# Making the pool of small columns ahead of the pools for weights in a two-block f32 kernel

## The chip, the cores and the metric

The kernel runs on one core of one Trainium2 chip (trn2). The metric is the device time of one execution in microseconds; it is given as the median of several runs. One execution was also taken by the hardware profiler, and every row below is from that one.

## The reference, cut to what matters

Sequence 512, model width 1024, all inputs and weights f32. A first block has an even layer (input projection, a 31-tap causal convolution, multi-scale pooling, output projection) and an odd layer (a gated linear recurrence over 12 heads of 128 channels). A second block has an S5 layer with a gated output projection, an MLP and a gated side input, then an attention layer with a window of 128 and a second MLP and side input. What matters here is that nearly all of it is matrix products of 512 tokens with weights that are used once:

```python
p = jnp.einsum("btd,dn->btn", h, w_in)                      # even and odd layer
y = jnp.einsum("btn,nd->btd", y, w_out)
ab = y @ w_glu                                              # S5 layer
h = h + jnp.square(jax.nn.relu(hm @ w_up[i])) @ w_down[i]   # both layers of the second block
gate = jax.nn.sigmoid(rmsnorm_2(h, norm_ple[i]) @ w_ple_gate[i])
```

## The kernel before

Activations lie in SBUF with channels on the 128 partitions and 512 tokens along the free dimension. To keep f32 accuracy with f32r matmuls, every activation and every weight is held as a pair `hi`, `lo` with hi + lo equal to the f32 value, and each product is three matmuls (`mm3`, L279 to L286): hi weights with the hi activation (L284), hi weights with the lo activation (L285), lo weights with the hi activation (L286). The weights are the stationary operand (128 columns of 4 bytes, so 512 bytes per partition) and the activation is streamed (512 columns, 2048 bytes per partition). One output tile of 128 channels with 1024 inputs is 8 times `mm3`, 24 matmuls on one PSUM bank (`mtile`).

Weights come in chunks of 128 x 1024 floats, in an order that `queue_w` lays down for the whole program. `prep` (L256 to L269) does one chunk: SP issues the DMA into a tile of pool `raw` (2 slots), ScalarE copies it to a tile of pool `whi` (tag `hi`, 3 slots, L266), and VectorE or GpSimd subtracts into a tile of pool `wlo` (tag `lo`, 3 slots, L268). `get_w` runs it up to three chunks ahead of the matmuls that use them.

SBUF is handed out by pools. Seven pools live for the whole program and are made in `Kern.__init__` (L171 to L178): `const`, `raw`, `whi`, `wlo`, `h` (the residual stream), `xg` (normed activations, 16 tiles of 2048 bytes) and `small` (columns of statistics: tags `v`, `rs`, `st`, `sm`, of 4 to 24 floats, 4 slots each). Pools lie one behind the other in the order in which they are made. Behind them each phase opens a pool of its own, whose tiles are made by `self.L(tag, ...)`; that pool is given back when the phase ends, and the next phase's pool begins at the same place. In the kernel before, the pools begin at these bytes of a partition:

| pool | begins at | size | remainder of its tiles by 512 |
|---|---|---|---|
| raw | 21056 | 8192 | 64 |
| whi | 29248 | 12288 | 64 |
| wlo | 41536 | 12288 | 64 |
| h | 53824 | 20480 | 64 |
| xg | 74304 | 32768 | 64 |
| small | 107072 | 1152 | - |
| phases | 108224 | - | by the tag, below |

The size of `small` is 4 slots of 32 + 64 + 96 + 96 bytes. All other pools of the list have sizes that are multiples of 512 bytes.

What each phase streams against the weights (the time is where it stands in the profiled execution):

- even layer, 0 to 430 us: `xg`, and from the phase's pool `big` and `d`
- odd layer, 430 to 722 us: `xg`, `xs` against two small weight tiles `wrh` and `wrl` of the same phase's pool, then `y` for its output projection
- S5, 722 to 806 us: small matmuls of 64 columns; the projections of the side inputs (`y`) fill PE's idle time
- gated output projection (`glu`), 806 to 892 us: `y`. Two of its sixteen chunks aren't in `whi` and `wlo` but, since L1251, in the phase's tiles `x` and `gt`
- MLP and, behind it, the side input with its gate (`ple`), twice (892 to 1294 us, and 1493 to 1897 us): products with `w_up` stream `xg`, those with `w_down` and `w_gate` stream `hid`; each half of the hidden width is 16 output tiles of `w_up`, then 8 of `w_down` with 2048 inputs each
- attention, 1294 to 1493 us: `xg`, then `o` for queries and part of the output projection; scores and values use `q`, `k`, `pt`, `vh`, `vl` of the phase's pool among themselves

PE runs its matmuls in program order; each phase's order is fixed when the program is built.

Of the kernel before, what the change touches and what calls it, by code (L numbers as in the profile page):

```python
# [37 lines left out]
class Vecs:  # L38
    def __init__(self):
        self.parts, self.at, self.n = [], {}, 0  # L40
# [116 lines left out]
class Kern:  # L157
# [10 lines left out]
    def __init__(self, ctx, tc, I, O, vat, cat):  # L168
        self.tc, self.nc, self.I, self.O = tc, tc.nc, I, O
        self.vat, self.cat = vat, cat  # L170
        P = lambda name, bufs, **k: ctx.enter_context(tc.tile_pool(name=name, bufs=bufs, **k))  # L171
        self.p_const = P("const", 1)
        self.p_raw = P("raw", 2)
        self.p_hi = P("whi", 3)
        self.p_lo = P("wlo", 3)
        self.p_h = P("h", 10)
        self.p_xg = P("xg", 16)
        self.p_s = P("small", 4)  # L178
        self.ps_st = P("stats", 1, space=PSUM)
        self.dram = P("dram", 1, space=bass.MemoryType.DRAM)  # L180
        self.chunks, self.prepped, self.next_prep, self.next_get = [], {}, 0, 0
# [1565 lines left out]
```

## Time and profile before

| | us |
|---|---|
| median of 3 runs | 1912.23 |
| lowest, highest | 1911.62, 1917.79 |
| the profiled execution's own time | 1913.36 |
| its span, from the first to the last instruction | 1911.6 |

The span is 1.8 us shorter than the time of the same execution. Times in the rows are microseconds, and the duration of a single instruction (mean) is in nanoseconds. A matmul's duration reaches from its start to the modelled end of its last result; matmuls overlap, so 24 matmuls that each last 390 ns take much less than 24 times 390 ns, and what a matmul costs in a dense stretch is the distance from its start to the next one's start. I call that distance its step. It can be read in two ways: from the starts in the timeline, or from a stretch in which PE is never idle, as the length of the stretch plus one duration, divided by the count of matmuls that touch it (the plus is for the ones that the stretch cuts at its ends). PEclk 1.00 is the full TensorE clock (2.4 GHz), 0.5 the lower level (1.2 GHz).

### The profile page before, as it was taken

The numbers are of one execution on the slowest core, as the hardware profiler recorded it, in microseconds if no ns is written. First come the engines' busy times: TensorE is split into PE (matmuls) and PEld (weight loads), VectorE is DVE, ScalarE is ACT, GpSimd is POOL, SyncE is SP. The second block draws the span as 40 slices with busy tenths as digits, with TensorE's granted clock in tenths as the row PEclk, the third lists the DMA queues.
The fourth block names the chain that finished last, engine by engine and source line by source line (L and its number), as shares of the span: only waits on it lengthen the run. The fifth ranks groups of instructions, "written<-read, shape, count | busy, mean of one in ns | idle before, by whom it ended". The sixth has DMA issues, their size and how long they took to land.

```text
span 1911.6 us, 23182 instructions
## 1 busy us (share of the span) xinstructions
PE 1777.6 (93%) x8530; PEld 1427.3 (75%) x8530; DVE 1256.9 (66%) x1940; ACT 751.2 (39%) x1274; POOL 573.4 (30%) x606
## 2 busy tenths in 40 slices
PE   6998989799988797799999999999999999999997
PEld 5776767567766675687888888887778888888886
DVE  8999999976778768755432344478776642244456
ACT  3334332443454553224432332334665432233234
POOL 4889877683657643200000000023000000000002
PEclk8999989898989898899999999999999999999998
DMA  4233333432212378623232222333111222222322
GB/s 151 85 112 98 101 100 117 119 95 90 75 63 88 110 238 279 203 77 111 93 99 89 100 99 89 100 105 111 49 54 45 100 99 89 98 100 90 98 88 94
DMA packets 104289, 200.57 MB, mean 105 GB/s; under 512 B 26736, under 2 KB 57072, under 8 KB 104176
## 3 DMA queue, kind: packets, MB, share of 16 engines
q1 hardware_dynamic: 96496, 182.41, 29.7%
q0 software_dynamic: 2640, 8.65, 1.4%
q10 hardware_dynamic: 5040, 8.04, 1.2%
q8 instruction: 67, 1.10, 0.2%
q14 instruction: 46, 0.38, 0.1%
HBM read 176.38 MB, written 22.02 MB: 104 GB/s over the span
## 4 chain that ended last, share of the span: by engine, by line
PE 62%; DVE 21%; issue 5%; POOL 5%; DMA 4%; ACT 3%; SPq 1%; ACTq 0%; POOLq 0%; DVEq 0%
PE mm L284 17%; PE mm L285 17%; PE mm L286 17%; DVE cv L240 7%; POOL lo L228 2%; DVE pl L228 1%; PE pv L1519 1%; DMA raw<-in_w_in_odd 1%; DVE srr L228 1%; ACT hi L225 1%; PE sc L284 1%; PE sc L285 1%; PE sc L286 1%; DVE xs L228 1%; DVE lo L228 1%
## 5 line engine op out<-in xcount | busy, mean ns | idle before, releaser
L225 ACT ACTIVATE hi<-raw 128x1024 fp32r<-128x1024 f32 (+1 forms) x280 | 292.5, 1047 | 674.8 <-PE mm L285 541.4
L228 DVE TENSOR_TENSOR lo<-raw,hi 128x1024 fp32r<-128x1024 f32 (+1 forms) x185 | 227.2, 1228 | 417.7 <-ACT hi L225 414.3
L286 PE MATMUL mm<-xg,lo 128*128 128x512 f32 x924 | 365.7, 396 | 5.6 <-POOL lo L228 5.6
L284 PE MATMUL mm<-xg,hi 128*128 128x512 f32 x924 | 366.4, 398 | 1.7 <-ACT xs L225 1.4
L285 PE MATMUL mm<-xg,hi 128*128 128x512 f32 x924 | 365.0, 396 | 0.0
L1333 POOL DMA_DIRECT2D pj<-proj x16 | 8.8, 549 | 1036.3 <-DVE t L240 795.7
L228 POOL TENSOR_TENSOR lo<-raw,hi 128x1024 fp32r<-128x1024 f32 (+1 forms) x95 | 233.5, 2460 | 127.0 <-ACT hi L225 116.3
L284 PE MATMUL mm<-hid,hi 128*128 128x512 f32 (+1 forms) x648 | 254.4, 393 | 1.4 <-DVE t L228 1.4
L285 PE MATMUL mm<-hid,hi 128*128 128x512 f32 (+1 forms) x648 | 253.9, 392 | 0.0
L286 PE MATMUL mm<-hid,lo 128*128 128x512 f32 (+1 forms) x648 | 253.8, 392 | 0.0
L286 PEld LDWEIGHTS mm<-xg,lo 128*128 128x128 f32 x924 | 176.4, 191 | 44.5 <-POOL lo L228 7.1
L284 PEld LDWEIGHTS mm<-xg,hi 128*128 128x128 f32 x924 | 176.6, 191 | 41.1 <-ACT xs L225 1.9
L285 PEld LDWEIGHTS mm<-xg,hi 128*128 128x128 f32 x924 | 176.7, 191 | 38.4 <-issue 1.2
L240 DVE SCALAR_TENSOR_TENSOR cv<-b,hw,cv 128x510 f32<-128x510 f32 (+28 forms) x232 | 159.0, 729 | 0.0
L284 PEld LDWEIGHTS mm<-hid,hi 128*128 128x128 f32 x648 | 121.7, 188 | 30.2 <-DVE t L228 1.6
L286 PEld LDWEIGHTS mm<-hid,lo 128*128 128x128 f32 x648 | 121.7, 188 | 28.6
L285 PEld LDWEIGHTS mm<-hid,hi 128*128 128x128 f32 x648 | 121.7, 188 | 28.5
L284 PE MATMUL mm<-y,hi 128*128 128x512 f32 x192 | 79.3, 413 | 8.9 <-ACT y L225 8.4
L285 PE MATMUL mm<-y,hi 128*128 128x512 f32 x192 | 77.5, 404 | 0.0
L286 PE MATMUL mm<-y,lo 128*128 128x512 f32 x192 | 77.0, 402 | 0.0
L285 PE MATMUL mm<-big,hi 128*128 128x512 f32 x160 | 67.8, 425 | 8.7 <-DVE big L240 7.9
L284 PE MATMUL mm<-big,hi 128*128 128x512 f32 x160 | 65.0, 425 | 5.3 <-DVE gt L240 3.0
(467 smaller groups left out, 3140.9 us busy)
## 6 DMA issues: line engine op xcount, KB each, us to landing
raw<-in_w_up SPq DMA_DIRECT2D x64, 512.0 KB
raw<-in_w_down SPq DMA_DIRECT2D x64, 512.0 KB
raw<-in_w_in_even SPq DMA_DIRECT2D x40, 512.0 KB
raw<-in_w_in_odd SPq DMA_DIRECT2D x24, 512.0 KB
raw<-in_w_out_even SPq DMA_DIRECT2D x16, 512.0 KB
raw<-in_w_glu SPq DMA_DIRECT2D x16, 512.0 KB
raw<-in_w_gate SPq DMA_DIRECT2D x16, 512.0 KB
raw<-in_w_out_odd SPq DMA_DIRECT2D x16, 384.0 KB
```

Source lines behind the costliest of these rows:

```text
L225: self.nc.scalar.activation(out=out, in_=in_, func=func, scale=scale, bias=bias)
L228: (eng or self.nc.vector).tensor_tensor(out=out, in0=a, in1=b, op=op)
L240: self.nc.vector.scalar_tensor_tensor(out=out, in0=a, scalar=s, in1=b, op0=op0, op1=op1)
L284: mm(out, hi[:, sl], xh, start=start, stop=False)
L285: mm(out, hi[:, sl], xl, start=False, stop=False)
L286: mm(out, lo[:, sl], xh, start=False, stop=stop)
L1333: self.nc.gpsimd.dma_start(out=p, in_=pj[m])
L1519: mm(o, l, r[:, w], start=n == 0, stop=n == 6 * nk - 1)
```

## The change

The line that makes the pool `small` moves from behind the pool `xg` to behind the pool `const`.

```diff
         self.p_const = P("const", 1)
+        self.p_s = P("small", 4)
         self.p_raw = P("raw", 2)
         self.p_hi = P("whi", 3)
         self.p_lo = P("wlo", 3)
         self.p_h = P("h", 10)
         self.p_xg = P("xg", 16)
-        self.p_s = P("small", 4)
         self.ps_st = P("stats", 1, space=PSUM)
```

No instruction is added, removed or moved in the code. `small` then begins where `raw` began, and `raw`, `whi`, `wlo`, `h` and `xg` begin 1152 bytes later, which is 2 x 512 + 128; the phases' pools begin at 108224 as before. The remainder by 512 of the tiles of these five pools goes from 64 to 192. That of the phases' tiles stays, by the sizes of what lies ahead of them in their pool: 192 for `xs`, `wrh`, `wrl`, `x`, `gt`, `y` and `hid`, 448 for `d` and `o`, 32 for `big`. Slices of a weight tile begin at multiples of 512 bytes in it, and streamed tiles are 2048 bytes each, so the distance between a streamed tile and a slice of weights has one remainder by 512 for each pair of tags:

| streamed | weights | before | after |
|---|---|---|---|
| xg | hi, lo | 0 | 0 |
| xs | wrh, wrl | 0 | 0 |
| y | x, gt | 0 | 0 |
| y | hi, lo | 128 | 0 |
| hid | hi, lo | 128 | 0 |
| d, o | hi, lo | 384 | 256 |
| big | hi, lo | 480 | 352 |

## Rows read from the trace of the kernel before

**Rows 1.** The page's first part: busy time, share of the span, instructions of each engine.
```profile
PE 1777.6 (93%) x8530; PEld 1427.3 (75%) x8530; DVE 1256.9 (66%) x1940; ACT 751.2 (39%) x1274; POOL 573.4 (30%) x606
```

**Rows 2.** Stretches by phase: busy us (instructions) of PE, PEld, DVE, ACT, POOL; clock; DMA.
```profile
0.00:430.00 430.00, 376.24 (x1621) 291.78 (x1622) 409.78 (x713) 165.72 (x343) 335.65 (x438) 0.93 0.35 109
...
638.00:722.00 84.00, 78.22 (x330) 61.86 (x329) 60.25 (x56) 39.38 (x55) 43.64 (x32) 0.96 0.64 201
722.00:806.00 84.00, 59.79 (x878) 48.83 (x879) 73.47 (x144) 20.24 (x37) 26.64 (x23) 0.86 0.78 253
806.00:892.00 86.00, 84.65 (x378) 68.45 (x374) 36.51 (x45) 25.01 (x33) 1.65 (x3) 1.00 0.28 94
...
981.00:1071.00 90.00, 90.00 (x388) 72.40 (x387) 20.91 (x18) 21.80 (x26) 0.00 (x0) 1.00 0.30 94
1071.00:1158.00 87.00, 87.00 (x385) 72.07 (x384) 39.27 (x46) 34.23 (x48) 0.00 (x0) 1.00 0.29 97
...
1294.00:1493.00 199.00, 190.16 (x1048) 153.84 (x1048) 150.67 (x329) 118.40 (x311) 16.43 (x15) 0.98 0.21 68
```

**Rows 3.** Waits of ScalarE, 978 to 1296 us: total us, times, longest.
```profile
ACT hi L225 <- PE mm L285: 173.7, 50, 4.6
```

**Rows 4.** PE alone, inside stretches of one streamed tag: length, busy (matmuls), clock, DMA.
```profile
985.00:1065.00 80.00, 80.00 (x345) 1.00 0.31 97
1075.00:1155.00 80.00, 80.00 (x354) 1.00 0.28 95
...
1590.00:1670.00 80.00, 80.00 (x344) 1.00 0.29 94
1675.00:1755.00 80.00, 80.00 (x355) 1.00 0.29 99
...
825.00:885.00 60.00, 60.00 (x260) 1.00 0.31 106
```

**Rows 5.** Groups by line and form, 806.5 to 890.6 us: count, busy us, mean ns.
```profile
L285 PE MATMUL mm<-y,hi 128*128 128x512 f32 x105 | 41.4, 395 | 0.0
...
L285 PE MATMUL sp<-y,x 128*128 128x512 f32 x8 | 3.1, 390 | 0.0
L285 PE MATMUL sp<-y,gt 128*128 128x512 f32 x8 | 3.1, 390 | 0.0
```

**Rows 6.** Timeline of PE, first and last of 24 matmuls in a row, and the next.
```profile
817.66 0.39 PE L284 MATMUL sp<-y,x 128*128 128x512 f32 x1
...
822.88 0.40 PE L286 MATMUL sp<-y,gt 128*128 128x512 f32 x1
823.11 0.40 PE L284 MATMUL mm<-y,hi 128*128 128x512 f32 x1
```

**Rows 7.** Groups by line and form, PE, whole span: count, busy us, mean ns, idle.
```profile
L284 PE MATMUL mm<-hid,hi 128*128 128x512 f32 x632 | 249.8, 395 | 0.0
...
L285 PE MATMUL mm<-y,hi 128*128 128x512 f32 x192 | 77.5, 404 | 0.0
...
L285 PE MATMUL mm<-big,hi 128*128 128x512 f32 x160 | 67.8, 425 | 8.7 <-DVE big L240 7.9 <-DVE big L228 0.8
...
L285 PE MATMUL mm<-o,hi 128*128 128x512 f32 x56 | 22.0, 394 | 0.0
...
L285 PE MATMUL sc<-o,hi 128*128 128x512 f32 x40 | 15.9, 398 | 0.0
...
L285 PE MATMUL sp<-y,hi 128*128 128x512 f32 x24 | 10.4, 433 | 0.0
...
L285 PE MATMUL yp<-y,hi 128*128 128x512 f32 x24 | 9.5, 395 | 0.0
...
L285 PE MATMUL mm<-d,hi 128*128 128x512 f32 x16 | 6.3, 393 | 0.0
L284 PE MATMUL mm<-hid,hi 128*128 128x256 f32 x16 | 4.6, 289 | 1.4 <-DVE t L228 1.4
```

**Rows 8.** Chain of waits, 638 to 722 us: shares by line.
```profile
by line: issue 7.3%; DMA raw<-in_w_proj 7.0%; PE sp L286 6.4%; DVE e L733 6.0%; POOL lo L228 5.8%; PE sp L284 5.6%; PE sp L285 5.4%; PE mm L286 5.0%; PE yp L285 5.0%; PE yp L286 5.0%; PE mm L285 5.0%; PE yp L284 5.0%; PE mm L284 5.0%; ACT x
```

## The prediction

> **What bounds the kernel now.** I read the page's busy times first, then the stretches phase by phase, then the waits, and last the steps of single matmuls. PE is busy 93% of the span [rows 1], but that is an average over phases with different limits [rows 2]. In the even layer (0 to 430 us) PE is busy 376 of 430 us while VectorE is busy 410: VectorE sets the pace there. In S5 (722 to 806 us) PE is idle 24 of 84 us. From 806 us on it is otherwise: in the gated output projection PE is busy 84.7 of 86 us, in the stretches of the MLPs 90.0 of 90 and 87.0 of 87 us at the full clock of 2.4 GHz, with VectorE at a quarter to a half of its time. There the time of the kernel is the count of matmuls times the step from one to the next. Nothing else is late: ScalarE, which makes the `hi` weights, mostly waits for PE to give a weight buffer back, 173.7 us between 978 and 1296 us [rows 3]. So weights lie ready ahead of PE, and a PE with a shorter step finishes sooner.
>
> The step isn't the same everywhere. I take stretches in which only one streamed tag runs and PE has no idle time [rows 4]. With `hid` streamed, 345 and 344 matmuls touch 80 us; with `xg`, 354 and 355. A matmul lasts about 0.39 us, so the step is (80 + 0.39)/345 = 233.0 ns and 80.39/344 = 233.7 ns for `hid`, 233.4 ns on average, and 227.1 and 226.5 ns, 226.8 on average, for `xg`. Same form of matmul, same weight pools, same clock, about the same DMA rate (94 to 99 GB/s): 6.6 ns apart, in both layers. For `y` in 825 to 885 us it is 60.39/260 = 232.3 ns.
>
> What tells `hid` and `y` from `xg` is, by the table of the change, the distance to the weights: a multiple of 512 bytes for `xg`, 128 more for the others. The trace has a control inside one phase: in the gated output projection 48 matmuls stream `y` against weights that lie in `x` and `gt`, at a multiple of 512. Twenty-four of them in a row start between 817.66 and 822.88 us [rows 6]: 23 steps in 5.22 us, 227.0 ns. Right behind them the same tiles of `y` against `hi` and `lo` go at 232.3 ns. The durations say the same: 390 ns against `x` and `gt`, 395 against `hi` [rows 5]. So it isn't the streamed tile, and since `xg` goes at 226.8 with `hi` and `lo`, it isn't the weights' pool either; it is the pair.
>
> **The change part by part.** It removes and adds no instruction, wait or buffer, and moves none past a queue: sizes of pools, and so the reuse of their slots, stay. It moves five pools by 1152 bytes. What that can change is what depends on addresses; I price it by streamed tag.
>
> `hid`: 632 matmuls on each of three lines [rows 7], 1896, go from a distance of 128 to 0. If they take the step of `xg`: 1896 x 6.6 ns = 12.5 us. All of it lies on the path, since PE is never idle there [rows 2]. If they gain only what `y` shows between its two kinds of weights, 232.3 - 227.0 = 5.3 ns, it is 10.0 us. I take 12.5, from the stretches of the same kind and length, and keep 10.0 for the range.
>
> `y`: 3 x (192 + 24 + 24) = 720 matmuls against `hi` and `lo` [rows 7], also from 128 to 0. In the gated output projection 105 per line [rows 5], 315 x 5.3 ns = 1.7 us, on the path since PE has 1.4 us of idle time in 86. In 638 to 722 us PE runs 330 matmuls, nearly all of them `y`: 312 x 5.3 ns = 1.6 us at most. But PE is idle 5.8 of 84 us there, the clock is 0.96, and the chain of waits has loads of weights with 7% and GpSimd's `lo` with 6% [rows 8], which don't get shorter, so 0 to 1.6; I take the middle, 0.8. The rest, 720 - 315 - 312 = 93, fills idle time of PE in S5: nothing.
>
> `xg`, `xs`, and `y` against `x` and `gt` keep the distance 0: nothing.
>
> `o`, `d` and `big` change from one distance that isn't 0 to another: 384 to 256, 384 to 256, 480 to 352. No row shows 256 or 352. The rows nearest to them are those at 128 and 384: `o` lasts 394 ns and `d` 393, `hid` 395 [rows 7], so the penalty hardly depends on the distance once there is one, and I take 0. From both sides: `o` has 3 x (56 + 40) = 288 matmuls, which could lose the whole penalty or pay it twice, 288 x 6.6 ns = 1.9 us either way. `big` has 3 x 160 and `d` 3 x 16, 528 x 6.6 ns = 3.5 us, but in a phase where VectorE sets the pace, so at most half, 1.7 us either way.
>
> VectorE, ScalarE and GpSimd also read and write tiles that move against each other, such as `h` against the phases' tiles; the pair that they handle most, `raw` with `hi` into `lo`, moves together and keeps its distances. No row lets me price the others; where it would count, behind 806 us, these engines have slack [rows 2], so 0.
>
> Sum: 12.5 + 1.7 + 0.8 = 15.0 us. The profiled execution took 1913.4 us, so 1898.4; it stands 1.1 us above the median of the runs, 1912.2, and from that it is 1897.2 us. Ends: 12.5 + 1.7 + 1.6 + 1.9 + 1.7 = 19.4 us gained, 1892.8; and 10.0 + 1.7 + 0 - 1.9 - 1.7 = 8.1 us gained, 1904.1. With a microsecond for the spread of the runs: 1892 to 1905.
>
> **A rule that speaks against it.** In this trace the same `y` tiles go at 227.0 ns against one set of weights and at 232.3 against the other [rows 4, 6], so what the weights are, or where they lie, reaches into the step of the streaming matmul. The Trainium skill, TensorE: Matmul & The Clock Gate, section Step-by-step: what each phase is for, says that PE has two independent read ports into SBUF, one for the streamed operand and one for the weight load, and that loading the next weights takes no read bandwidth from the running matmul. By that rule a distance between the two addresses would be worth nothing and the time would stay at 1912; the rows don't agree with it by 5 to 7 ns a matmul.
>
> **The rivals.** First, *the pair matters, but not by the remainder of 512*. All pairs at 227 ns are also near neighbours in SBUF (`xg` with `hi` and `lo`, `y` with `x` and `gt`), all slow pairs lie farther apart; a slower step for far tiles would fit rows 4 to 6 as well. The change leaves far tiles far: the sum is 0 and the time 1912. Nothing in the rows rules it out; against it is only that the penalty would have to step once at some place and then stay flat. The skill's rule of independent ports ends at the same time.
>
> Second, on the other side, *what counts is where a tile lies by itself*: tiles of `raw` to `xg` at remainder 64 are the good ones, and the change takes them to 192. Then `xg` against `hi` and `lo` would go from 226.8 to 233.4 ns: `w_up` alone has 2 layers x 32 tiles x 24 = 1536 matmuls in stretches where PE is never idle, 1536 x 6.6 ns = 10.1 us, and the time would be 1922. It decides from the first `w_up` tile on. Against it: `y`, `x` and `gt` all lie at 192 and go at 227.0 ns [rows 6].
>
> Third, *the gain on `hid` is given back*: with steps of 227 ns a chunk of weights is used up in 24 x 227 = 5.4 us instead of 5.6, and loads or conversions become late. Against it: the stretches of `xg` use chunks at just that rate, with VectorE busy 39 of 87 us instead of 21 of 90, and PE stays at 87.0 of 87 [rows 2]. Were most of the 12.5 us eaten, the time would be about 1908.
>
> **How the numbers follow.** The forecast has 0.87; the rival of near and far 0.06, with no change; the weights that come late 0.03, also inside 0.3%; tiles by themselves 0.04, slower. 0.3% is 5.7 us, about what a measurement of this kernel can tell from no change; the forecast's whole range lies beyond it. So faster 0.87, same 0.09, slower 0.04. The range of the forecast holds nearly all of its 0.87, and I leave the rivals' times out of it.
>
> **What would show it.** Right, if in the profile of the changed kernel 80 us inside a stretch of `hid` hold 353 to 355 matmuls, with 389 or 390 ns each, the stretches of `xg` still hold 354, the 24 matmuls against `x` and `gt` still take 5.2 us and those behind them the same step; and if the even layer and attention end as late after their start as now, within 2 us. Wrong, if `hid` stays at 344, or if `xg` falls to 344, or if PE shows idle time inside a stretch of `hid`.

## The result and the profile after

The changed kernel takes 1901.11 us (median, 1900.59 to 1902.89) where the kernel before takes 1911.92 beside it: a ratio of 0.9936, with a 95% interval of 0.9918 to 0.9953. It was timed twice more, each time beside the kernel before: 0.9953 (0.9936 to 0.9970; 1904.50 against 1915.36 us) and, in five rounds, 0.9929 (0.9917 to 0.9941; 1902.78 against 1916.24 us). So it is faster by 0.5 to 0.7%, by the ratios 9 to 14 us. Forecast were 15.0 us and 1897.2, with a range of 1892 to 1905. Ratios leave out executions in a slow state, of which there was one in all the runs below (4376.7 us, with the gap of 128 bytes). All engines run the same instructions in the same order in both kernels; only addresses differ.

First the stretches of PE inside one streamed tag, which answer to [rows 4]: length, busy time (matmuls), clock, DMA. The first, third and fourth are `hid`, the second and fifth `xg`, and the last, from the gated output projection, `y`.

```profile
985.00:1060.00 75.00, 75.00 (x333) 1.00 0.30 97
1075.00:1145.00 70.00, 70.00 (x311) 1.00 0.29 98
1165.00:1240.00 75.00, 75.00 (x333) 1.00 0.30 96
1580.00:1655.00 75.00, 75.00 (x332) 1.00 0.31 99
1670.00:1740.00 70.00, 70.00 (x310) 1.00 0.28 98
...
825.00:885.00 60.00, 60.00 (x267) 1.00 0.31 106
```

By the same reading as before, `hid` has a step of 75.39/333 = 226.4 and 75.39/332 = 227.1 ns, where it had 233.0 and 233.7. `xg` stays: 70.39/311 = 226.3 and 70.39/310 = 227.1 ns. `y` goes from 232.3 to 60.39/267 = 226.2 ns. The groups of the gated projection (807 to 889 us; count, busy us, mean ns), which answer to [rows 5], show it in the durations: `y` against `hi` now lasts as long as against `x` and `gt`.

```profile
L285 PE MATMUL mm<-y,hi 128*128 128x512 f32 x103 | 40.1, 389 | 0.0
...
L285 PE MATMUL sp<-y,x 128*128 128x512 f32 x8 | 3.1, 389 | 0.0
...
L285 PE MATMUL sp<-y,gt 128*128 128x512 f32 x8 | 3.1, 389 | 0.0
```

Then the timeline of PE, the matmuls that answer to [rows 6]: 23 steps from 819.24 to 824.45 us, 226.5 ns, where it was 227.0. But the last of them starts 1.57 us later than before (822.88).

```profile
819.24 0.39 PE L284 MATMUL sp<-y,x 128*128 128x512 f32 x1
...
824.45 0.39 PE L286 MATMUL sp<-y,gt 128*128 128x512 f32 x1
824.68 0.39 PE L284 MATMUL mm<-y,hi 128*128 128x512 f32 x1
```

Where the time went is read from the starts of the blocks. Of the kernel before, the first `hid` of the first MLP, the first `xg` behind it, the next first `hid`, and the first matmul of attention:

```profile
981.15 0.40 PE L284 MATMUL mm<-hid,hi 128*128 128x512 f32 x1
...
1070.74 0.39 PE L284 MATMUL mm<-xg,hi 128*128 128x512 f32 x1
...
1157.79 0.40 PE L284 MATMUL mm<-hid,hi 128*128 128x512 f32 x1
...
1293.81 0.39 PE L284 MATMUL sc<-xg,hi 128*128 128x512 f32 x1
```

The same four of the changed kernel:

```profile
981.09 0.39 PE L284 MATMUL mm<-hid,hi 128*128 128x512 f32 x1
...
1068.12 0.39 PE L284 MATMUL mm<-xg,hi 128*128 128x512 f32 x1
...
1155.16 0.39 PE L284 MATMUL mm<-hid,hi 128*128 128x512 f32 x1
...
1287.61 0.39 PE L284 MATMUL sc<-xg,hi 128*128 128x512 f32 x1
```

From each to the next: 89.59 us of `hid` become 87.03, 87.05 us of `xg` stay 87.04, and 136.02 us of `hid` become 132.45. The second MLP repeats it (89.59 and 87.04). The whole account of the profiled executions, from starts of blocks in the timelines:

| part | before, us | after, us | difference |
|---|---|---|---|
| start to the first `y` of the odd layer's output projection | 638.19 | 640.26 | +2.07 |
| from there to the last of the 24 matmuls of [rows 6] | 184.69 | 184.19 | -0.50 |
| the rest of the gated output projection, 300 of its 336 matmuls against `hi` and `lo` | 69.22 | 67.58 | -1.64 |
| `w_up`, four blocks together | 352.09 | 352.06 | -0.03 |
| `w_down` of the first halves, two blocks | 179.18 | 174.07 | -5.11 |
| `w_down` of the second half and side input, first MLP | 136.02 | 132.45 | -3.57 |
| attention | 199.39 | 200.29 | +0.90 |
| `w_down` of the second half, side input and the end, to the last matmul | 144.99 | 142.41 | -2.58 |

The sum is -10.5 us. The rows with `hid` and the gated projection together give 12.9; 2.5 are lost ahead of the 24 matmuls and in attention.

### The profile page after: what moved, and what is told of

Its sections match the earlier page's. It is cut to its first block, busy times and chain, and to the rows that moved or that the text cites. A ratio compares the mean times of both kernels' runs of the same rounds, so it can differ in the third digit from the quotient of the medians.

```text
span 1901.1 us, 23182 instructions
## 1 busy us (share of the span) xinstructions
PE 1758.7 (93%) x8530; PEld 1425.8 (75%) x8530; DVE 1259.9 (66%) x1940; ACT 749.7 (39%) x1274; POOL 571.0 (30%) x606
## 4 chain that ended last, share of the span: by engine, by line
PE 57%; DVE 23%; issue 6%; DMA 5%; POOL 4%; ACT 3%; SPq 1%; ACTq 0%; DVEq 0%; POOLq 0%
PE mm L284 17%; PE mm L285 16%; PE mm L286 16%; DVE cv L240 7%; POOL lo L228 2%; DVE pl L228 1%; DMA raw<-in_w_in_odd 1%; PE pv L1519 1%; SPq L1085 1%; DVE srr L228 1%; ACT hi L225 1%; DVE e L733 1%; PE sc L284 1%; PE sc L285 1%; PE sc L286 1%
## 5 line engine op out<-in xcount | busy, mean ns | idle before, releaser
L286 PE MATMUL mm<-xg,lo 128*128 128x512 f32 x924 | 364.8, 395 | 6.4 <-POOL lo L228 6.4
L284 PE MATMUL mm<-xg,hi 128*128 128x512 f32 x924 | 365.4, 397 | 1.5 <-ACT xs L225 1.5
L285 PE MATMUL mm<-xg,hi 128*128 128x512 f32 x924 | 363.8, 395 | 0.0
L284 PE MATMUL mm<-hid,hi 128*128 128x512 f32 (+1 forms) x648 | 250.7, 387 | 1.8 <-DVE t L228 1.8
L285 PE MATMUL mm<-hid,hi 128*128 128x512 f32 (+1 forms) x648 | 250.3, 387 | 0.0
L286 PE MATMUL mm<-hid,lo 128*128 128x512 f32 (+1 forms) x648 | 250.1, 386 | 0.0
L286 PEld LDWEIGHTS mm<-xg,lo 128*128 128x128 f32 x924 | 175.9, 190 | 45.1 <-POOL lo L228 7.9
L284 PEld LDWEIGHTS mm<-xg,hi 128*128 128x128 f32 x924 | 176.1, 191 | 40.4 <-ACT xs L225 1.9
L285 PEld LDWEIGHTS mm<-xg,hi 128*128 128x128 f32 x924 | 175.9, 190 | 38.2 <-issue 1.2
L284 PEld LDWEIGHTS mm<-hid,hi 128*128 128x128 f32 x648 | 121.7, 188 | 26.6 <-DVE t L228 2.0
L286 PEld LDWEIGHTS mm<-hid,lo 128*128 128x128 f32 x648 | 121.7, 188 | 24.7
L285 PEld LDWEIGHTS mm<-hid,hi 128*128 128x128 f32 x648 | 121.7, 188 | 24.6
L284 PE MATMUL mm<-y,hi 128*128 128x512 f32 x192 | 77.7, 405 | 10.5 <-ACT y L225 9.3
L286 PE MATMUL mm<-y,lo 128*128 128x512 f32 x192 | 75.7, 395 | 1.7 <-POOL lo L228 1.7
L285 PE MATMUL mm<-big,hi 128*128 128x512 f32 x160 | 68.5, 429 | 8.6 <-DVE big L240 7.6
L285 PE MATMUL mm<-y,hi 128*128 128x512 f32 x192 | 75.7, 394 | 0.0
L284 PE MATMUL mm<-big,hi 128*128 128x512 f32 x160 | 65.7, 429 | 10.1 <-DVE gt L240 5.8
```

Source lines behind the costliest of these rows:

```text
L284: mm(out, hi[:, sl], xh, start=start, stop=False)
L285: mm(out, hi[:, sl], xl, start=False, stop=False)
L286: mm(out, lo[:, sl], xh, start=False, stop=stop)
```

## The experiments

**Undoing the distance alone, and repeating both kernels.** The theory of the prediction was that the pair of a streamed tile and weights costs nothing extra at a multiple of 512 bytes. Its rivals were near and far tiles, and tiles that are good by their own place. The profile after speaks against near and far by itself: `hid` is as far from `hi` as before. To tell the pair from the place, a gap behind `xg` brings the old distances back while the weights stay at their new place:

```diff
-        self.p_xg = P("xg", 16)
+        self.p_xg = P("xg", 16); P("gap", 1).tile([128, 32], F32, name="gap")   # 128 bytes
```

> The changed kernel with a gap of 128 bytes behind xg, so that the phases' pools begin 128 bytes later: every streamed tag has the remainder by 512 to hi and lo that it had in the kernel before (y and hid 128, o and d 384, big 480), while raw to xg lie where the change put them. If the remainder of the distance is the cause: hid and y go back to a step of 232 to 234 ns and 395 ns of duration, the time to within 2 us of the kernel before if moving the low pools costs nothing by itself ('spread'), or to 2 to 4 us above it ('moved pools'). If it were the place of the low pools by itself that helped (any pair with hi at its new place is fast): hid stays at 227 ns and the time at 1901.

The ratio to the kernel before is 1.0006 (0.9988 to 1.0024): all of the gain is gone. In 985 to 1055 us, stretch and groups:

```profile
985.00:1055.00 70.00, 70.00 (x301) 1.00 0.30 94
```

```profile
L285 PE MATMUL mm<-hid,hi 128*128 128x512 f32 x101 | 39.9, 395 | 0.0
```

70.39/301 = 233.9 ns and 395 ns, as before. So it is the distance, and not where the weights lie; nor is it where `hid` lies by itself, which the change left at the same place (remainder 192) and made faster.

The later start of the gated projection was the open point. Both kernels were run again unchanged.

> The changed kernel as it is, once more, beside the kernel before. In its first profile the stretches of hid gained 12 us as forecast, but the matmuls of S5 and of the gated projection began 1.8 us later than in the kernel before (3.5 to 4.2 us later in the even layer), and attention took about 1 us more. Theory 'spread': this is how far two executions of one kernel differ in the phases where VectorE sets the pace; then the start of the gated projection (805.9 us before, 807.7 us after) comes out anywhere within 804 to 809 us this time, and the ratio of times stays 0.992 to 0.996. Theory 'moved pools': moving raw, whi, wlo, h and xg costs 2 to 4 us in the even layer; then the gated projection starts at 807.5 to 809 us again.

> The kernel before as it is, for one more profile. 'Spread': the start of the gated projection's matmuls differs from 805.9 us by some microseconds, as between the first profiles of before and after. 'Moved pools': it is within 0.5 us of 805.9.

The first matmul of the gated projection started at 806.45 us in the first profile of the kernel before and at 806.95 in the second; in the changed kernel at 808.21, then 808.44, and in a third profile (below) at 804.92. Taken alone, both repetitions fit the moved pools. But the third profile starts 3.5 us earlier than the second with the same program, and the version with the gap of 128, whose low pools lie just as in the changed kernel, at 805.69. At 240 us, in the even layer, two executions of the very same kernel before were 3.0 us apart (the same matmul at 238.78 and 241.77 us), and by 600 us they were level again within 0.1 us. There single VectorE instructions differ: the same one on 12 columns lasts 0.60 us in one execution and 2.37 in the other. So what was seen lies within the spread between executions in the phases that VectorE leads. A cost of the moved pools of a microsecond or so can't be excluded by this.

**Which distances are good.** In the changed kernel `o` lies at a distance of 256, and its groups against `hi` and `lo` in the bank `sc` had become shorter, 394, 389 and 393 ns after 398, 394 and 397. So other gaps were put in the same place, of 256, 32 and 64 bytes.

> The changed kernel with a gap of 256 bytes behind xg: y and hid lie 256 from hi and lo by 512, o and d at 0, big at 96. If only distances of a multiple of 512 are good: hid at 232 to 234 ns, 395 ns each, and the time 12 to 14 us above the changed kernel. If multiples of 256 are good too, as the duration of o in the changed kernel hints (389 to 394 ns in its second group at a distance of 256, where it had 394 to 398 at 384): hid at 227 ns, and the time of the changed kernel within 2 us.

The ratio is 0.9945 (0.9924 to 0.9967), in a second run of five rounds 0.9928 (0.9914 to 0.9942), where the changed kernel beside it had 0.9929. In 990 to 1060 us:

```profile
990.00:1060.00 70.00, 70.00 (x310) 1.00 0.32 98
```

```profile
L286 PE MATMUL mm<-hid,lo 128*128 128x512 f32 x104 | 40.5, 390 | 0.0
```

70.39/310 = 227.1 ns: a multiple of 256 is as good as one of 512. A multiple of 512, by which the table of the change counts, asks for more than is needed.

> The changed kernel with a gap of 32 bytes behind xg: y and hid lie 32 from hi and lo by 256. If any remainder by 256 other than 0 costs the same (128, 384 and 480 did, by 5 to 8 ns): hid at 232 to 234 ns, 395 ns each. If the cost grows with the remainder: hid between 227 and 230 ns.

> The changed kernel with a gap of 64 bytes behind xg: y and hid at a remainder of 64. If what counts is 256: hid at 232 to 234 ns. If it were 64 (all that was slow so far but 32, 96 and 480 would then have been fast, and 128 was slow): 227 ns.

The same stretch with 32 bytes, then with 64, and with 64 its three lines:

```profile
990.00:1060.00 70.00, 70.00 (x302) 1.00 0.30 91
```

```profile
990.00:1060.00 70.00, 70.00 (x308) 1.00 0.32 98
```

```profile
L284 PE MATMUL mm<-hid,hi 128*128 128x512 f32 x103 | 40.6, 394 | 0.0
L286 PE MATMUL mm<-hid,lo 128*128 128x512 f32 x103 | 40.4, 392 | 0.0
L285 PE MATMUL mm<-hid,hi 128*128 128x512 f32 x102 | 39.6, 388 | 0.0
```

With 32 the step is 70.39/302 = 233.1 ns, the whole penalty, and the one execution took 1913.1 us. With 64 it is 70.39/308 = 228.5 ns, and the lines differ: L285 has none of it, L284 most. Neither expectation named that: 64 costs a quarter to a third of the penalty (the block of 384 `hid` matmuls takes 87.9 us, where it takes 87.0 in the changed kernel and 89.6 in the kernel before). The one execution took 1907.8 us. So the penalty isn't flat, as the prediction took it to be: it is whole at 32 and at 128 and small at 64. Nor does the remainder alone settle it there: with `y`, at the same 64, it is L284 that has none (388 ns in 830 to 880 us), and L285 and L286 last 392 and 394. Why, no run shows.

**Own weights or the next ones.** While a matmul streams, the weights of the next are loaded; so it stands in the timeline of the kernel before, where PEld is the engine that loads weights:

```profile
1020.34 0.40 PE L284 MATMUL mm<-hid,hi 128*128 128x512 f32 x1
1020.34 0.19 PEld L285 LDWEIGHTS mm<-hid,hi 128*128 128x128 f32 x1
1020.58 0.39 PE L285 MATMUL mm<-hid,hi 128*128 128x512 f32 x1
1020.58 0.19 PEld L286 LDWEIGHTS mm<-hid,lo 128*128 128x128 f32 x1
```

To tell which of the two tiles matters, `lo` alone was displaced:

```diff
-        self.p_lo = P("wlo", 3)
-        self.p_h = P("h", 10)
+        P("gap", 1).tile([128, 32], F32, name="gap"); self.p_lo = P("wlo", 3)
+        P("gap2", 1).tile([128, 96], F32, name="gap2"); self.p_h = P("h", 10)
...
-        s = self.p_s.tile([128, 24], F32, tag="st", name="st_s")
+        s = self.p_s.tile([128, 24], F32, tag="st", name="st_s", bufs=1)
```

> The changed kernel with the lo weights alone displaced: a gap of 128 bytes ahead of wlo and one of 384 behind it, and the tag st of the small pool with one slot (it is used once). xg, y and hid lie at 0 to hi and at 384 to lo by 512. In the order L284 (hi), L285 (hi), L286 (lo) the weights that are loaded while L285 streams are lo, and while L286 streams hi. If the pair that counts is a matmul and the load of the next weights: L285 at 232 to 234 ns and 395 ns, L284 and L286 at 227 ns and 389 or 390 ns. If it is a matmul and its own weights: L286 slow, L284 and L285 fast. Either way a third of the matmuls of xg, y and hid, some 2000 in the dense stretches counting both, loses 5 to 7 ns: hid (632) and xg of w_up (512) lose about 7 us, so 1908 to 1912.

It took 1917.31 us, 1.0012 (1.0002 to 1.0021) of the kernel before and more than the 1908 to 1912 expected. Its groups with `hid` (990 to 1060 us) and with `xg` (1085 to 1140 us):

```profile
L286 PE MATMUL mm<-hid,lo 128*128 128x512 f32 x102 | 40.5, 397 | 0.0
L285 PE MATMUL mm<-hid,hi 128*128 128x512 f32 x102 | 40.4, 396 | 0.0
L284 PE MATMUL mm<-hid,hi 128*128 128x512 f32 x101 | 39.3, 389 | 0.0
...
L286 PE MATMUL mm<-xg,lo 128*128 128x512 f32 x80 | 31.8, 397 | 0.0
L285 PE MATMUL mm<-xg,hi 128*128 128x512 f32 x80 | 31.7, 396 | 0.0
L284 PE MATMUL mm<-xg,hi 128*128 128x512 f32 x80 | 31.1, 389 | 0.0
```

Both expectations fell: two lines of three are slow, not one. They are L285, which has good weights of its own and a displaced load behind it, and L286, which is the other way round. That left two theories, which differ in what `hi` displaced instead of `lo` would do (the same gaps, one pool earlier):

> The mirror of the run with the lo weights displaced: now hi lies 128 off and lo at 0 (a gap of 128 bytes ahead of whi, one of 384 behind it, the tag st with one slot). There L285 (own weights hi at 0, next load lo at 384) and L286 (own lo at 384, next load hi at 0) were both slow, 396 and 397 ns, and L284 (hi, then hi again) was fast, so neither the next load alone nor the own weights alone decides. Theory 'either': a matmul is slow when its own or the next weights are off; then all three lines are slow here, 394 to 397 ns, and the step is 232 to 234 ns in hid and xg alike. Theory 'change': it is slow where own and next weights have different remainders; then L285 (hi, next lo) and L286 (lo, next hi) are slow and L284 is fast although both its weights are off by 128, 389 ns.

```profile
L285 PE MATMUL mm<-hid,hi 128*128 128x512 f32 x101 | 39.9, 395 | 0.0
L286 PE MATMUL mm<-hid,lo 128*128 128x512 f32 x100 | 39.7, 397 | 0.0
L284 PE MATMUL mm<-hid,hi 128*128 128x512 f32 x101 | 39.7, 393 | 0.0
```

All three are slow, in `hid` and in `xg` alike (393, 395 and 397 ns there too): a matmul is slow when its own weights or the next ones are off. The one execution took 1927.2 us, beside 1916.2 for the kernel before. That is also the price of losing `xg`, which the second rival put at 10.1 us: the four `w_up` blocks took 362.0 us, 9.9 more than before. By which path its own weights, loaded a step earlier, still reach the step, no run shows.

**Aligning the rest.** Three gaps inside phases' pools bring `big`, `d` and `o` to 0 as well:

```diff
-        hw = self.L("hw", 1, F32, (128, 8 * KC))
+        hw = self.L("hw", 1, F32, (128, 8 * KC)); self.L("gap", 1, F32, (128, 40))
...
-                v = self.L("v", 2)
+                v = self.L("v", 2); len(ds) + c == 1 and self.L("gap2", 1, F32, (128, 24))
...
-        idb = self.L("idb", 1, BF16, (128, 128))
+        idb = self.L("idb", 1, BF16, (128, 128)); self.L("gap3", 1, F32, (128, 64))
```

> The changed kernel with gaps of 160, 96 and 256 bytes inside three phases' pools, so that big, d and o too lie at 0 to hi and lo by 512. big goes from 233 to 227 ns (480 matmuls, 2.9 us of PE time), but in the even layer VectorE sets the pace: 0 to 1.5 us. d: 48 matmuls, 0. o went from 384 to 256 with the change and 256 is as good as 512: 0. Time 0 to 2 us below the changed kernel, about 1901 to 1903 where before is 1912 to 1914, ratio to before 0.992 to 0.995. If the even layer hung on PE after all, up to 3 us.

Five rounds gave 0.9923 (0.9909 to 0.9938). To set it beside the changed kernel, both and the gap of 256 were timed once more on one chip.

> The changed kernel, timed in five rounds for the size of the effect: ratio to the kernel before 0.992 to 0.996, 1901 to 1905 us where before is 1912 to 1915. The step in hid gives 1896 x 6.6 = 12.5 us and the gated projection 1.7; a microsecond of it is lost where the clock falls once more in attention or at the end, if it does.

> The version with big, d and o aligned too, beside the changed kernel on the same chip: 0 to 2 us below it (the first run of it had 0.9923 of before, the changed kernel 0.9945 in a run of its own and 0.9953 in another). If the even layer follows VectorE alone, no difference; if some of big's 480 matmuls are on the path, 1 to 3 us.

> The version with y and hid at 256 instead of 0, beside the changed kernel: if 256 is as good as 512, the same time within 1.5 us. If the profile that was 5 us shorter in the even layer and S5 showed something of the layout and not of the execution, 3 to 5 us below the changed kernel.

It was 0.9929 (0.9917 to 0.9941) for the changed kernel, 0.9924 (0.9911 to 0.9937) with everything aligned, 0.9928 (0.9914 to 0.9942) with 256: no difference is seen. (The two profiled executions with 256 were both short, spans of 1896.1 and 1895.9 us; the timed runs don't follow them, so it is not a gain of that layout.) The step of `big` did fall, from 233 to 228 ns by the starts at the full clock, which is 2.4 us over its 480 matmuls. That nothing of it shows in the time fits the forecast that VectorE leads in the even layer, but 2.4 us is also about as wide as these intervals, so it is not shown that none of it is on the path. No version found here beats the changed kernel.

## Why the prediction was right, and where it missed

*What bounds the kernel*: right for the MLPs and the gated projection, where the steps of the matmuls are the time. PE waited for nothing between 978 and 1290 us in the changed kernel either, and the rival of late weights didn't come.

*`hid`*: right in mechanism and size. A block of 384 matmuls lost 89.59 - 87.03 = 2.56 us, 6.7 ns each, where 6.6 were forecast. Over all `hid` blocks, the last one up to its last matmul of 512 columns (130.20 us became 126.77), that is 5.11 + 3.57 + 3.43 = 12.1 us against 12.5 forecast. The reading from stretches of the same kind was the right choice over the 5.3 ns from `y`.

*`y`*: in the gated projection 1.64 us and, in the 30 matmuls ahead of those against `x` and `gt`, 0.15 more, against 1.7 forecast (for 315 matmuls; there are 336). The 0.8 us for the odd layer's output projection was not found: its 312 matmuls took 82.1 and 82.5 us in two profiles of the kernel before and 84.2, 83.1 and 83.7 in three of the changed kernel. If a part of it was on the path, the spread hides it.

*`o`*: taken at 0, with 1.9 us either way. The step fell where 0 was taken, since 256 is a good distance; in the dense run of 78 `o` matmuls that ends attention it gave 0.4 us (18.24 us became 17.83). The guess rested on rows at 128 and 384, that is, on the premise that all distances other than 0 are alike by 512.

*Attention and the end*: this is the term that was missing, about 2 us. Attention took 200.29 us instead of 199.39 although its `o` matmuls got shorter. Every profile has a fall of the granted clock where attention begins (0.66 in 1300 to 1310 us before); the changed kernel's has a second one. Length, busy time (matmuls), clock and DMA of 1350 to 1360 us in the changed kernel, and of the same stretch before:

```profile
1350.00:1360.00 10.00, 9.30 (x45) 0.83 0.19 60
```

```profile
1350.00:1360.00 10.00, 9.04 (x46) 1.00 0.15 47
```

PE, which waits for others at the head of attention (it is busy 9.3 of these 10 us, and 8.6 of the 10 ahead of 1340), fell to the lower level of 1.2 GHz for a part of it: 0.83 on average. In the repetition of the changed kernel it was 0.83 from 1340 to 1350 us, and attention took 201.3 us; in the third profile there is no second fall, and it took 199.2. The second fall doesn't need the shorter step: it came with the gap of 32, where `hid` is slow, and in one of the two profiles with everything aligned (201.2 us with it, 198.9 without). So it is part of the spread, and worth more than the 0.4 us of `o`.

At the end of the kernel part of the gain is given back in every profile of the changed kernel. The last `hid` block ends with matmuls of 256 columns, in two halves, and the second half waits for VectorE; before, then after:

```profile
1893.62 0.39 PE L284 MATMUL mm<-hid,hi 128*128 128x256 f32 x1 [1.36 <-DVE t L228]
...
1882.71 0.39 PE L284 MATMUL mm<-hid,hi 128*128 128x256 f32 x1 [1.78 <-DVE t L228]
```

PE waits 0.4 us longer there (1.77 us in the two later profiles too), and the last small matmuls take 0.4 us more; over the 3.5 us up to the last one the clock was 0.50, where it was 0.59 before. From the last `hid` matmul of 512 columns to the last matmul it is 15.6 us, 14.8 before. In the second and third profile it is 16.9, where the clock was also low in an earlier stretch (0.66 in 1884 to 1889 us of the second).

*The sum*: 15.0 us forecast, 10.8 in the first comparison and 13.5 in the longest one, inside the range. In the profiled pair `hid` and the gated projection gave 13.9 us of the 14.2 forecast for them. What the sum put at nothing took 3.5 back in this pair: 0.9 in attention, 0.9 at the end, and 1.7 ahead of the gated projection, where the 0.8 of `y` should have come. The 1.7 lies within the spread that the repetitions show, for which the range allowed one microsecond, where the kernel before alone ran from 1909.8 to 1919.9 us over the comparisons. So the step was forecast rightly, and 1897.2 was too low by what lies outside the dense stretches, part of it chance.

*The rivals*: near and far tiles would have left `hid` slow, and tiles by their own place would have slowed `xg`; `hid` became fast and `xg`, now at remainder 192, stayed at 226.3 and 227.1 ns. The Trainium skill, TensorE: Matmul & The Clock Gate, section Step-by-step: what each phase is for, has PE read the streamed operand and the weights through two independent ports; by that rule the time would have stayed at 1912. The run with the gap of 128 bytes disagrees with it: its ratio is 1.0006 with one set of distances, where that of the changed kernel is 0.993 to 0.995 with the other, and nothing else changed but those. What the weight loads and the stream share, no run shows.

## What to carry to other kernels

Where a phase is bound by a dense stream of matmuls, measure the step in it by streamed tag: two tags with the same form and clock that differed by 3% pointed at addresses here. It is worth knowing the addresses of the tiles then, and keeping streamed tiles and weights of f32r matmuls at distances that are multiples of 256 bytes. Here one pool whose size is no multiple of that, lying between them, lost 0.5 to 0.7%, and moving it showed no cost beyond the spread. In the even layer, where VectorE sets the pace, aligning showed no gain. And a gain on a dense stretch may be given back where the next wait is for another engine, as at the end of this kernel.

## What the runs showed of the hardware

- The step of a 128 x 512 f32r matmul at the full clock was 227 ns with weights at 0 or 256 bytes, by 512, from the streamed tile, 233 to 234 ns at 32 and 128, and 228.5 to 229 ns at 64; the durations were 389 or 390, 395, and 388 to 394 ns. At 384, with `o`, they were 394 to 395 ns in the dense run.
- Both the weights in use and those loaded next count: with `lo` displaced, 389, 396 and 397 ns for the three lines; with `hi` displaced, 393, 395 and 397.
- Two executions of the same program were 3 us apart after 240 us of the even layer, where VectorE leads, and level again by 600 us; 3 us is a quarter of the effect studied here.
